# Group norm of a hybrid encoder: one square root for four token tiles, the middle tiles' statistics inside the last recurrence chunk, the bias folded into the bonus, and one more half gate in chunk 0

## The chip, the cores and the metric

The kernel runs on one core of one Trainium2 chip. The metric is the device time of one execution in microseconds (us), median of three runs. Five engines work beside each other, each through its own list of instructions in order: TensorE (PE in the rows, its weight loads PEld), VectorE (DVE), ScalarE (ACT), GpSimd (POOL) and SyncE (SP, which here only starts DMA transfers).

## The reference, cut to what matters

One encoder layer over 512 tokens of width 1024, in float32. The part that the change touches is the end of branch A, an RWKV-7 recurrence in both directions with 8 heads of 64 channels:

```python
y = rwkv7_scan(..., False) + rwkv7_scan(..., True)      # (tokens, heads, 64)
mean = jnp.mean(y, axis=-1, keepdims=True)
var = jnp.mean(jnp.square(y - mean), axis=-1, keepdims=True)
y = ((y - mean) * lax.rsqrt(var + GN_EPS)).reshape(B, S, W)
y = y * ln_w + ln_b
bonus = jnp.sum(jnp.sum(r_h[:, :, None] * k_dir * r_k, axis=-1, keepdims=True), axis=2) * v_h
y = (y + bonus.reshape(B, S, W)) * g                     # g = sigmoid(gd) @ g2
y_a = y @ w_o
merged = sigmoid(gate_A) * y_a + sigmoid(gate_B) * y_b   # y_b: differential attention
```

Behind it come the output projection, a feed-forward part of width 4096 and a gated embedding part.

## The kernel before

Products of float32 matrices are done in three matmuls of a split form (`whi`, `wlo` are the two halves of a weight unit of 128x1024; ACT makes the first at line 131, DVE the second at line 135). Weight units are loaded ahead, in order, into 3 raw and 4 split buffers.

The work runs in stages. **Preparation** (lines 297 to 551): projections of the input (`in`), and for each of four head pairs p and two directions d a chain from `zw`, `za` (matmuls) over ACT functions and DVE products (`ga`, `ae`, `bk`) to matmuls `aps` that need `bk`, and at the end of each p the bonus `bv` (line 536), which goes to DRAM as `bvd` and comes back later as `bvt`. The next stage's first matmuls (`da`) fill PE's waits from the last pair on. **Attention** follows with the first half of the gates (`gA`) and its projection (`yb`).

**The recurrence** (lines 1052 to 1154) works in 8 chunks of 64 tokens, both directions in step. A chunk has the matmuls `al`, a copy `B` by ACT and DVE, `ss` with B, a copy `srv` by ACT and DVE, `ss` with srv, the update of the state `S` by DVE, and `yy`, whose result is stored in `ya` (chunks 0 to 3, by ACT) or added to it (chunks 4 to 7, by DVE, line 1109). In the list of PE each small group waits for the copies before it. To give PE something in these waits, halves of the second gates `gB` (8 gates of 24 matmuls each, halves of 12) are put between by `fill`; a gate that is complete is drained on DVE and ACT (`gb`, line 1122; tanh; `mB`, line 1124), and the split of a further weight unit comes along with it:

```python
for i in range(NCH):
    steps = [step(i, d) for d in range(2)]
    for st_ in range(6):
        for g in steps:
            next(g)
        if st_ == 0 or (i, st_) == (0, 2):
            fill(1)
```

So 9 halves lie in the chunks, 2 of them in chunk 0, and the other 7 behind them (line 1200), where they run beside the group norm.

**The group norm** (lines 1164 to 1198) goes over four token tiles of 128: sum, mean, difference, square on ACT, sum, square root on ACT, reciprocal, product, and four transposes into `yps`. Then for each of four channel tiles: `yf` from yps with the scale `lnw` and the bias `lnb` on ACT (line 1191), the bonus added on DVE (line 1192), the product with the output gate `gq` (a matmul), and the split into `ygh` and `ygl`. These feed the projection `ya` (line 1211, weight units `wo`), whose PSUM bank is one of two that the gates use too: the first `ya` needs the bank of gate 6 and the second that of gate 7, so both need those gates' `gb`. Rows of DVE that add to the tile named ya (line 1109) and matmuls named ya (projection, lines 245 to 247) are different things.

The order on each engine is set by a scheduler when the kernel is built, from the program's order and priorities and its own estimates of when things are ready; `issue_after` pins an instruction behind another one on its engine.

Of the kernel before, what the change touches and what calls it, by code (L numbers as in the profile page):

```python
# [10 lines left out]
F32 = mybir.dt.float32  # L11
F32R = mybir.dt.float32r
AF = mybir.ActivationFunctionType
ALU = mybir.AluOpType
AX = mybir.AxisListType

P = 128
T = 512
D = 1024
C = 64  # L20
NCH = T // C
# [88 lines left out]
class Weights:  # L110
# [34 lines left out]
    def next(self, *key):  # L145
        assert UNITS[self.cur] == key, (UNITS[self.cur], key)
        self.prefetch(1 + self.AHEAD)
        w = self.ready[self.cur]
        self.ready[self.cur] = None
        self.cur += 1  # L150
        return w
# [3 lines left out]
def tile_hybrid_encoder(ctx, tc, xT, wts, par, cst_a, cst_p, lor, lqk, nfin, out, dbg=None):  # L155
    nc = tc.nc
# [4 lines left out]
    def pool(name, bufs=1, side=None, space=None):  # L161
        kw = {"reuse_waits": "tile"} if space != DR else {}
        if side:
            kw["side"] = side
        if space is not None:
            kw["space"] = space
        return Pool(tc.tile_pool(name=name, bufs=bufs, **kw))

    def dump(name, t, idx=None):
        if name in dbg:  # L170
            o = dbg[name]
            nc.sync.dma_start(o if idx is None else o[idx], t)
# [17 lines left out]
    eps6, epsg, sub8, lam = [one[:, i:i + 1] for i in range(4)]  # L190
# [4 lines left out]
    def par_col(name, i):  # L195
        return pr[:, POFF[name] + i:POFF[name] + i + 1]
# [167 lines left out]
    def tmp(tag, name, bufs=1):  # L364
        return pp.tile([P, T], F32, tag=tag, name=name, bufs=bufs)
# [8 lines left out]
    def proj_in(f, dst):  # L374
        shifted(proj(f), f, dst)
# [70 lines left out]
    for p in range(4):  # L446
# [87 lines left out]
        nc.tensor.matmul(bps, cp[:, CP["blk"]:CP["blk"] + P], rk, start=True, stop=True)  # L534
        bv = tmp("bv", f"bv{p}")
        nc.vector.tensor_tensor(bv, bps, v_, ALU.mult)
        nc.sync.dma_start(bvd[p], bv)
    proj_in(14, sgd)
    nc.scalar.activation(sgd, sgd, AF.Tanh, scale=0.5)
# [170 lines left out]
    def gate(f, pool_, stops):  # L710

        w = W.next("in", 3456 + f * P)
        ps = psd.tile([P, T], F32, tag="d", name=f"gA{f}")
        for k in range(8):
            wk = slice(k * P, k * P + P)
            for i, (a, b) in enumerate(((0, hhi), (0, hlo), (1, hhi))):
                chained(nc.tensor.matmul, ps, w[a][:, wk], moved(b[:, k, :]), start=(k == 0 and i == 0), stop=(k == 7 and i == 2))
            if k in stops and k < 7:
                yield
        late.append((f, ps, pool_))  # L720
        yield
# [3 lines left out]
    def gated():  # L725

        while late:
            f, ps, pool_ = late.pop()
            go = pool_.tile([P, T], F32, tag="go", name=f"go{f}", bufs=1)
            K(nc.vector.tensor_tensor, go, ps, rbs, ALU.mult)  # L730
            K(nc.scalar.activation, go, go, AF.Tanh, scale=0.5)
            nc.sync.dma_start(gad_[f], go)
# [283 lines left out]
    yp = pool("yp", side="right")  # L1016
    ya = yp.tile([P, 4, 8, C], F32, name="ya")
    bvt = yp.tile([P, 4, T], F32, name="bvt")
    sq_ = pool("seq", side="right")
# [8 lines left out]
    seq_last = None  # L1028
# [83 lines left out]
    def gate_b(f):  # L1112

        nonlocal last_pe
        w = W.next("in", 4480 + f * P)
        ps = psd.tile([P, T], F32, tag="d", name=f"gB{f}")
        last_pe = dense_half(w, ps, 0)
        yield
        last_pe = dense_half(w, ps, 1)
        gb = yp.tile([P, T], F32, tag="gb", name=f"gb{f}", bufs=1)  # L1120
        m_ = mB[f // 4][:, f % 4, :]
        nc.vector.tensor_tensor(gb, ps, rbs, ALU.mult)
        nc.scalar.activation(gb, gb, AF.Tanh, scale=0.5)
        nc.vector.scalar_tensor_tensor(m_, gb, 1.0, m_, ALU.add, ALU.mult)
        yield

    def dense_work():
        for f in range(GA0, 8):
            for _ in gate(f, yp, (3, 7)):
                gated()  # L1130
                yield
        for f in range(8):
            yield from gate_b(f)

    def fill(n):

        nonlocal seq_last
        for _ in range(n):
            if seq_last is None:
                next(dense)  # L1140
            else:
                with tc.issue_after(seq_last.ins):
                    next(dense)
            seq_last = last_pe

    dense = dense_work()
    for i in range(NCH):
        steps = [step(i, d) for d in range(2)]
        for st_ in range(6):
            for g in steps:  # L1150
                next(g)
            if st_ == 0 or (i, st_) == (0, 2):
                fill(1)
    with tc.issue_after(last_chunk.ins):
        nc.gpsimd.dma_start(bvt, bvd.rearrange("a q t -> q a t"))
    pss.close_()
# [3 lines left out]
    sq_ = yp  # L1160
# [2 lines left out]

    psm = pool("psm2", bufs=6, space=PS)

    mean = sq_.tile([P, 4, 8], F32, name="mean")
    var = sq_.tile([P, 4, 8], F32, name="var")
    g2 = sq_.tile([P, 512], F32, name="g2")
    with tc.issue_after(last_chunk.ins):
        nc.gpsimd.dma_start(g2, lor[:, 2, :])  # L1170
    gps = []
    yps = [psm.tile([P, T], F32, tag="m", name=f"yps{p}") for p in range(4)]
    for tt in range(4):
        yt = ya[:, tt]
        nc.vector.tensor_reduce(mean[:, tt, :], yt, AX.X, ALU.add)
        nc.vector.tensor_scalar(mean[:, tt, :], mean[:, tt, :], 1.0 / C, None, ALU.mult)
        nc.vector.tensor_tensor(yt, yt, mean[:, tt, :, None].broadcast_to([P, 8, C]), ALU.subtract)
        yq = sq_.tile([P, 8, C], F32, tag="yq", name=f"yq{tt}", bufs=2)
        nc.scalar.activation(yq, yt, AF.Square)
        nc.vector.tensor_reduce(var[:, tt, :], yq, AX.X, ALU.add)  # L1180
        nc.scalar.activation(var[:, tt, :], var[:, tt, :], AF.Sqrt, bias=epsg, scale=1.0 / C)
        nc.vector.reciprocal(var[:, tt, :], var[:, tt, :])
        nc.vector.tensor_tensor(yt, yt, var[:, tt, :, None].broadcast_to([P, 8, C]), ALU.mult)
        for p in range(4):
            nc.tensor.transpose(yps[p][:, tt * P:(tt + 1) * P], yt[:, 2 * p:2 * p + 2, :].rearrange("q h e -> q (h e)"), ident)
# [2 lines left out]
    ygl = mg.tile([P, 4, T], F32R, name="ygl")  # L1188
    for p in range(4):
        yf = sq_.tile([P, T], F32, tag="yf", name=f"yf{p}", bufs=2)  # L1190
        nc.scalar.activation(yf, yps[p], AF.Identity, bias=par_col("lnb", p), scale=par_col("lnw", p))
        nc.vector.tensor_tensor(yf, yf, bvt[:, p, :], ALU.add)
        gq = psm.tile([P, T], F32, tag="m", name=f"gq{p}")
        nc.tensor.matmul(gq, g2[:, p * P:(p + 1) * P], sgd, start=True, stop=True)
        nc.vector.tensor_tensor(yf, yf, gq, ALU.mult)
        dump("yg", yf, p)
        nc.scalar.activation(halves(ygh[:, p, :]), turns(yf), AF.Copy)
        nc.vector.tensor_tensor(halves(ygl[:, p, :]), turns(yf), halves(ygh[:, p, :].bitcast(F32)), ALU.subtract)
# [7 lines left out]
    for f2 in range(4):  # L1206
        w = W.next("wo", f2)
        for i in range(2):
            f = 2 * f2 + i
# [286 lines left out]
```

## Time and profile before

| what | us |
|---|---|
| median of 3 runs (lowest, highest) | 924.59 (922.39, 930.75) |
| the profiled execution: device time | 924.65 |
| the profiled execution: span of the trace | 922.5 |
| PE busy in the span | 879.3 |
| DVE busy | 572.0 |
| ACT busy | 430.7 |
| mean granted clock of PE (1 is full) | 0.985 |

The span is the time from the first to the last instruction; 2.1 us of the device time lie around it. Starts in the rows count from the beginning of the span. A bracket at the end of a row gives how long the engine stood idle before it and for what. A row of stretches gives start and end, the length, then busy time and in parentheses the number of instructions of PE, PEld, DVE, ACT and POOL, then PEclk, the busy share of the DMA engines, and GB/s. PEclk is the granted clock of PE: 1.00 is 2.4 GHz and 0.50 is 1.2 GHz.

### The profile page before, as it was taken

The page shows a single profiled execution, that of the slowest core. Times are in us where ns is not written, and L with a number is a line of the kernel's source. Part 1 is how long each engine was busy: PE and PEld are TensorE (multiplying, and loading weights), DVE is VectorE, ACT ScalarE, POOL GpSimd, SP SyncE. Part 2 cuts the span into 40 slices and gives each one's busy share as a digit, 9 for nine tenths or more (in the row PEclk, how much of TensorE's full clock was granted, in tenths as well). Part 3 has the DMA queues.
Part 4 walks back from the last instruction along what each step waited for, and adds up shares of the span by engine and source line. Part 5 has one row for each costly group of instructions (what it writes and reads, how often), then busy time and mean ns, then how long its engine had stood idle before and what let it go on. Part 6 is the DMA issues. An engine that isn't in the chain of part 4 may idle for free.

```text
span 922.5 us, 14089 instructions
## 1 busy us (share of the span) xinstructions
PE 879.3 (95%) x5640; PEld 738.1 (80%) x5640; DVE 572.0 (62%) x873; ACT 430.7 (47%) x677; POOL 57.2 (6%) x84
## 2 busy tenths in 40 slices
PE   5999898899999998999999999999999999999995
PEld 3788777788567787888877888888888888888884
DVE  7756999759996624567887655553454345435453
ACT  6665555453587534321654554542243234214555
POOL 5000000020000031332000000000000000000000
PEclk9999999999999999998999999999999999999998
DMA  6534787796237263786136223233232323233502
GB/s 216 190 115 148 249 271 259 244 358 209 92 148 176 82 178 115 260 256 230 47 107 224 91 92 111 95 101 106 95 111 93 114 92 114 92 108 98 206 24 91
DMA packets 64720, 138.57 MB, mean 150 GB/s; under 512 B 25808, under 2 KB 28112, under 8 KB 62352
## 3 DMA queue, kind: packets, MB, share of 16 engines
q1 hardware_dynamic: 59424, 110.68, 36.6%
q0 software_dynamic: 5232, 27.01, 8.8%
q8 instruction: 44, 0.72, 0.3%
q14 instruction: 20, 0.16, 0.1%
HBM read 106.73 MB, written 30.93 MB: 149 GB/s over the span
## 4 chain that ended last, share of the span: by engine, by line
PE 69%; DVE 16%; ACT 7%; DMA 4%; issue 3%; SPq 1%; POOLq 0%; DVEq 0%; ACTq 0%
PE f L246 12%; PE f L247 12%; PE f L245 12%; PE gA L655 4%; DVE wlo L135 2%; PE yb L655 2%; PE ss L1037 2%; PE yy L1037 2%; PE sc L655 2%; PE ov L655 2%; DMA md<-ga 1%; PE wout L246 1%; DVE mi L580 1%; ACT whi L131 1%; PE wout L245 1%
## 5 line engine op out<-in xcount | busy, mean ns | idle before, releaser
L131 ACT ACTIVATE whi<-raw 128x1024 fp32r<-128x1024 f32 x134 | 141.4, 1057 | 284.1 <-PE f L246 183.4
L135 DVE TENSOR_TENSOR wlo<-raw,whi 128x1024 fp32r<-128x1024 f32 x134 | 166.9, 1248 | 49.4 <-ACT whi L131 48.8
L247 PE MATMUL f<-fh,wlo 128*128 128x512 f32 x256 | 97.2, 380 | 0.0
L245 PE MATMUL f<-fh,whi 128*128 128x512 f32 x256 | 97.1, 379 | 0.0
L246 PE MATMUL f<-fl,whi 128*128 128x512 f32 x256 | 97.1, 379 | 0.0
L247 PE MATMUL f<-h1h,wlo 128*128 128x512 f32 x256 | 97.0, 379 | 0.0
L245 PE MATMUL f<-h1h,whi 128*128 128x512 f32 x256 | 97.0, 379 | 0.0
L246 PE MATMUL f<-h1l,whi 128*128 128x512 f32 x256 | 97.0, 379 | 0.0
L1273 DVE TENSOR_TENSOR x<-x,f 128x512 f32<-128x512 f32 x32 | 22.0, 688 | 89.5 <-PE f L247 89.5
L1262 DVE SCALAR_TENSOR_TENSOR ft<-f,rf 128x512 f32<-128x512 f32 x32 | 22.2, 693 | 62.8 <-PE f L247 62.7
L245 PE MATMUL in<-hhi,whi 128*128 128x512 f32 x128 | 50.8, 397 | 6.8 <-ACT whi L131 6.8
L245 PEld LDWEIGHTS f<-h1h,whi 128*128 128x128 f32 x256 | 48.4, 189 | 6.9
L246 PEld LDWEIGHTS f<-h1l,whi 128*128 128x128 f32 x256 | 48.4, 189 | 6.9
L247 PEld LDWEIGHTS f<-h1h,wlo 128*128 128x128 f32 x256 | 48.4, 189 | 6.9
L246 PEld LDWEIGHTS f<-fl,whi 128*128 128x128 f32 x256 | 48.4, 189 | 6.8
L245 PEld LDWEIGHTS f<-fh,whi 128*128 128x128 f32 x256 | 48.4, 189 | 6.8
L247 PEld LDWEIGHTS f<-fh,wlo 128*128 128x128 f32 x256 | 48.4, 189 | 6.8
L246 PE MATMUL in<-hlo,whi 128*128 128x512 f32 x128 | 51.2, 400 | 2.4 <-DVE hlo L301 2.4
L247 PE MATMUL in<-hhi,wlo 128*128 128x512 f32 x128 | 50.5, 395 | 1.1 <-DVE wlo L135 1.1
L245 PEld LDWEIGHTS in<-hhi,whi 128*128 128x128 f32 x128 | 25.4, 198 | 10.4 <-ACT whi L131 6.8
L1265 DVE TENSOR_TENSOR h1l<-ft,h1h 128x512 fp32r<-128x512 f32 x32 | 27.1, 846 | 8.1 <-ACT h1h L1264 8.1
L246 PEld LDWEIGHTS in<-hlo,whi 128*128 128x128 f32 x128 | 25.0, 195 | 8.1 <-DVE hlo L301 4.8
(365 smaller groups left out, 1835.5 us busy)
## 6 DMA issues: line engine op xcount, KB each, us to landing
raw<-in_wts_dram SPq DMA_DIRECT2D x134, 512.0 KB, 3.5
gad<-ga SPq DMA_DIRECT2D x16, 1024.0 KB, 5.6
sga<-gad POOLq DMA_DIRECT2D x16, 1024.0 KB, 7.8
xs<-in_xT_dram SPq DMA_DIRECT2D x8, 256.0 KB, 5.5
ppd<-pps SPq DMA_DIRECT2D x2, 1024.0 KB, 5.7
md<-ga SPq DMA_DIRECT2D x32, 64.0 KB, 4.8
gates<-go SPq DMA_DIRECT2D x8, 256.0 KB, 2.2
mi<-md POOLq DMA_DIRECT2D x1, 2048.0 KB, 11.6
```

What stands on the lines that cost most here:

```text
L131: a = nc.scalar.activation(hi, raw, AF.Copy)
L135: b = nc.vector.tensor_tensor(lo, raw, hi.bitcast(F32), ALU.subtract)
L245: nc.tensor.matmul(ps, lh, moved(rh), start=first, stop=False)
L246: nc.tensor.matmul(ps, lh, moved(rl), start=False, stop=False)
L247: return nc.tensor.matmul(ps, ll, moved(rh), start=False, stop=last)
L580: behind[e] = f(*args, **kw)
L655: last_pe = f(*args, **kw)
L1037: seq_last = nc.tensor.matmul(*args, **kw)
L1262: nc.vector.scalar_tensor_tensor(t_, ps, 0.0, rf, ALU.max, ALU.mult)
L1265: nc.vector.tensor_tensor(halves(hl_[:, f, :]), turns(t_), halves(hh_[:, f, :].bitcast(F32)), ALU.subtract)
L1273: nc.vector.tensor_tensor(x[:, f, :], x[:, f, :], ps, ALU.add)
```

## The change

Four things are done:

- The bias `lnb` is added to the bonus `bv` by ACT during preparation, before it goes to DRAM. Then scale and bonus are one DVE instruction (line 1210 of the changed kernel) in place of an ACT and a DVE instruction.
- The statistics (sum, mean, difference, square, sum of squares) of the middle token tiles 1 and 2, which are complete after chunk 5, are put into the program inside chunk 7; those of tiles 0 and 3 come after the chunks.
- One square root and one reciprocal serve all four tiles, where there were four of each.
- A third half of a gate lies in chunk 0, behind the step in which `srv` is copied; so 6 halves, and not 7, are left behind the chunks.

```diff
         bv = tmp("bv", f"bv{p}")
         nc.vector.tensor_tensor(bv, bps, v_, ALU.mult)
+
+        nc.scalar.activation(bv, bv, AF.Identity, bias=par_col("lnb", p))
         nc.sync.dma_start(bvd[p], bv)
...
+    mean = yp.tile([P, 4, 8], F32, name="mean")
+    var = yp.tile([P, 4, 8], F32, name="var")
+    yqs = {}
+
+    def statistics(tt, part):
+
+        yt = ya[:, tt]
+        if part == 0:
+            nc.vector.tensor_reduce(mean[:, tt, :], yt, AX.X, ALU.add)
+            nc.vector.tensor_scalar(mean[:, tt, :], mean[:, tt, :], 1.0 / C, None, ALU.mult)
+        elif part == 1:
+            nc.vector.tensor_tensor(yt, yt, mean[:, tt, :, None].broadcast_to([P, 8, C]), ALU.subtract)
+            yqs[tt] = yp.tile([P, 8, C], F32, tag="yq", name=f"yq{tt}", bufs=2)
+            nc.scalar.activation(yqs[tt], yt, AF.Square)
+        else:
+            nc.vector.tensor_reduce(var[:, tt, :], yqs[tt], AX.X, ALU.add)
...
-            if st_ == 0 or (i, st_) == (0, 2):
+            if st_ == 0 or (i, st_) in ((0, 2), (0, 3)):
                 fill(1)
+            if i == NCH - 1 and st_ in (2, 3, 4):
+
+                with tc.issue_after(seq_last.ins):
+                    for tt in (1, 2):
+                        statistics(tt, st_ - 2)
...
+    for part in range(3):
+        for tt in (0, 3):
+            statistics(tt, part)
+    nc.scalar.activation(var, var, AF.Sqrt, bias=epsg, scale=1.0 / C)
+    nc.vector.reciprocal(var, var)
     for tt in range(4):
         yt = ya[:, tt]
-        nc.vector.tensor_reduce(mean[:, tt, :], yt, AX.X, ALU.add)
...
-        nc.scalar.activation(var[:, tt, :], var[:, tt, :], AF.Sqrt, bias=epsg, scale=1.0 / C)
-        nc.vector.reciprocal(var[:, tt, :], var[:, tt, :])
         nc.vector.tensor_tensor(yt, yt, var[:, tt, :, None].broadcast_to([P, 8, C]), ALU.mult)
...
-        nc.scalar.activation(yf, yps[p], AF.Identity, bias=par_col("lnb", p), scale=par_col("lnw", p))
-        nc.vector.tensor_tensor(yf, yf, bvt[:, p, :], ALU.add)
+        nc.vector.scalar_tensor_tensor(yf, yps[p], par_col("lnw", p), bvt[:, p, :], ALU.mult, ALU.add)
```

On PE in chunk 0, before (digits behind a name are chunk and direction, or the gate's number; the number after the underscore is the tile's): 

```order
L1037 MATMUL ss00_3339<-B00_3317,stt0_3266 64x64 x8
L1037 MATMUL ss01_3351<-B01_3320,stt0_3266 64x64 x8
L1037 MATMUL ss00_3339<-srv00_2570,sga00_2280 64x64 x8
L1037 MATMUL ss01_3351<-srv01_2572,sga01_2282 64x64 x8
L1037 MATMUL yy00_3350<-srv00_2570,sga00_2280 64x64 x8
L1037 MATMUL yy01_3362<-srv01_2572,sga01_2282 64x64 x8
```

And now, on PE at the same place; the dots stand for the remaining ten matmuls of the half gate:

```order
L1039 MATMUL ss00_3345<-B00_3323,stt0_3270 64x64 x8
L1039 MATMUL ss01_3357<-B01_3326,stt0_3270 64x64 x8
L245 MATMUL gB1_3375<-hhi_79,whi43_3224 128x512
L246 MATMUL gB1_3375<-hlo_80,whi43_3224 128x512
...
L1039 MATMUL ss00_3345<-srv00_2574,sga00_2284 64x64 x8
L1039 MATMUL ss01_3357<-srv01_2576,sga01_2286 64x64 x8
```

Half of gate 1 has moved between the two groups of ss. Its second half follows at the start of chunk 1, so gates are now complete at the start of chunks 1, 3, 5 and 7, and no longer of 2, 4 and 6.

On DVE in chunk 6, before, from the additions of chunk 5 to the second copy srv:

```order
L1109 TENSOR_TENSOR ya_3258<-yy51_4099,ya_3258 64x4x64 x2
L1122 TENSOR_TENSOR gb3_4175<-gB3_4015,rbs_143 128x512
L1175 TENSOR_REDUCE mean_4441<-ya_3258 128x8 x2
L1124 SCALAR_TENSOR_TENSOR mB0_3134<-gb3_4175,mB0_3134 128x512
L1073 COPY B60_4213<-al60_4179 64x4x64
L1073 COPY B61_4216<-al61_4196 64x4x64
L1176 TENSOR_SCALAR mean_4441<-mean_4441 128x8 x2
L135 TENSOR_TENSOR wlo49_4556<-raw49_4554,whi49_4555 128x1024
L1081 COPY srv60_4154<-ss60_4219 64x4x64
L1177 TENSOR_TENSOR ya_3258<-ya_3258,mean_4441 128x512
L1081 COPY srv61_4160<-ss61_4239 64x4x64
```

And now, on DVE at the same place:

```order
L1111 TENSOR_TENSOR ya_3262<-yy51_4121,ya_3262 64x4x64 x2
L1156 TENSOR_REDUCE mean_3284<-ya_3262 128x8 x2
L1157 TENSOR_SCALAR mean_3284<-mean_3284 128x8 x2
L1159 TENSOR_TENSOR ya_3262<-ya_3262,mean_3284 128x512
L1075 COPY B60_4238<-al60_4204 64x4x64
L1159 TENSOR_TENSOR ya_3262<-ya_3262,mean_3284 128x512
L1075 COPY B61_4241<-al61_4221 64x4x64
L1083 COPY srv60_4176<-ss60_4244 64x4x64
L1163 TENSOR_REDUCE var_3285<-yq1_4440 128x8
```

The scheduler takes the middle tiles' statistics out of chunk 7 up into chunk 6, among the copies that PE waits for there; the drain of a gate and a weight split have left this chunk, and stand before the copies of chunk 7 now (gb, wlo and mB, in this order).

On PE in the last piece of preparation (pair 3, direction 1), before; the dots stand for fifteen further da matmuls:

```order
L362 MATMUL za31_1476<-lx_266,lwl_264 128x512
L247 MATMUL da01_1689<-whi21_1665,hlo_80 128x512
L245 MATMUL da00_1688<-whi21_1665,hhi_79 128x512
...
L246 MATMUL da01_1689<-wlo22_1672,hhi_79 128x512
L247 MATMUL da01_1689<-whi22_1671,hlo_80 128x512
L517 MATMUL aps3100_1507<-ga310_1497,bk31_1496 128x128
```

And now; the dots stand for five further da matmuls:

```order
L362 MATMUL za31_1479<-lx_266,lwl_264 128x512
L245 MATMUL da01_1693<-whi22_1675,hhi_79 128x512
L246 MATMUL da01_1693<-wlo22_1676,hhi_79 128x512
...
L246 MATMUL da01_1693<-wlo22_1676,hhi_79 128x512
L247 MATMUL da01_1693<-whi22_1675,hlo_80 128x512
L517 MATMUL aps3100_1510<-ga310_1500,bk31_1499 128x128
```

Through the added ACT instruction the scheduler's order of the preparation changes as well: projections and the first 48 da matmuls stand earlier among the waits of PE (33 and 31 dense matmuls before the two aps of pair 1, where there were 26 and 24), and 9, not 19, are left for the last wait.

## Rows read from the trace of the kernel before

**Rows 1.** The page, busy time of each engine and its share of the span:

```profile
PE 879.3 (95%) x5640; PEld 738.1 (80%) x5640; DVE 572.0 (62%) x873; ACT 430.7 (47%) x677; POOL 57.2 (6%) x84
```

**Rows 2.** Busy times by stretch: most of the preparation:

```profile
88.00:166.00 78.00, 70.66 (x466) 57.24 (x465) 76.77 (x126) 46.43 (x91) 0.00 (x0) 1.00 0.76 249
```

**Rows 3.** Timeline of PE: chunk 0's wait; starts of chunks 2, 3, 4, 6, 7; chunk 6's wait:

```profile
366.24 1.15 PE L1037 MATMUL ss<-srv,sga 128*64 128x64 f32 x32 [2.44 <-DVE srv L1081]
...
381.71 0.68 PE L1037 MATMUL al<-srv,sga 64*64 64x64 f32 x16
...
392.21 0.68 PE L1037 MATMUL al<-srv,sga 64*64 64x64 f32 x16
...
401.84 0.68 PE L1037 MATMUL al<-srv,sga 64*64 64x64 f32 x16
...
422.34 0.68 PE L1037 MATMUL al<-srv,sga 64*64 64x64 f32 x16
...
426.54 1.10 PE L1037 MATMUL ss<-B,stt 64*64 64x64 f32 x14 [0.99 <-DVE B L1073]
...
436.62 0.68 PE L1037 MATMUL al<-srv,sga 64*64 64x64 f32 x16
```

**Rows 4.** Timeline of DVE in chunk 0, a gate's drain ahead of the copies:

```profile
362.93 0.69 DVE L1122 TENSOR_TENSOR gb<-gB,rbs 128x512 f32<-128x512 f32 x1 [1.94 <-PE gB L247]
363.81 1.22 DVE L135 TENSOR_TENSOR wlo<-raw,whi 128x1024 fp32r<-128x1024 f32 x1 [0.18 <-ACT whi L131]
```

**Rows 5.** Timeline of DVE at the start of chunk 6: additions, then two sums:

```profile
421.80 1.73 DVE L1109 TENSOR_TENSOR ya<-yy,ya 64x256 f32<-64x256 f32 x4
...
424.16 1.27 DVE L1175 TENSOR_REDUCE mean<-ya 128x8 f32<-128x512 f32 x2
```

**Rows 6.** Stretches around waits of PE, with its granted clock:

```profile
172.00:178.00 6.00, 4.00 (x22) 3.22 (x22) 4.78 (x9) 3.24 (x7) 0.00 (x0) 1.00 0.96 322
245.00:250.00 5.00, 3.27 (x12) 1.63 (x11) 4.54 (x9) 2.88 (x6) 0.00 (x0) 0.91 0.79 248
250.00:255.00 5.00, 5.00 (x21) 3.33 (x20) 4.82 (x13) 3.60 (x10) 0.00 (x0) 0.75 0.19 78
428.00:432.00 4.00, 4.00 (x74) 3.77 (x72) 2.02 (x5) 0.43 (x2) 0.00 (x0) 0.50 1.01 379
```

**Rows 7.** Timeline of PE behind the chunks: gate matmuls, then the first two projections:

```profile
442.53 0.48 PE L245 MATMUL gB<-hhi,whi 128*128 128x512 f32 x1
...
443.07 0.38 PE L247 MATMUL gB<-hhi,wlo 128*128 128x512 f32 x1
443.28 0.38 PE L245 MATMUL gB<-hhi,whi 128*128 128x512 f32 x1
...
466.13 0.38 PE L245 MATMUL ya<-ygh,whi 128*128 128x512 f32 x1
...
470.44 0.48 PE L245 MATMUL ya<-ygh,whi 128*128 128x512 f32 x1 [1.24 <-DVE gb L1122]
```

**Rows 8.** Timeline of ACT in the group norm, a table load and the roots behind it:

```profile
446.49 1.15 ACT L1179 ACTIVATE yq<-ya 128x512 f32<-128x512 f32 x2 [0.22 <-DVE ya L1177]
447.65 1.28 ACT L1181 ACT_TABLE_LOAD   x1
448.95 0.49 ACT L1181 ACTIVATE var<-var,one 128x8 f32<-128x8 f32 x2
```

**Rows 9.** Groups of DVE by line, shapes apart: the group norm's instructions:

```profile
L1198 DVE TENSOR_TENSOR ygl<-yf,ygh 128x512 fp32r<-128x512 f32 x4 | 3.0, 802 | 0.4 <-ACT ygh L1197 0.4
...
L1192 DVE TENSOR_TENSOR yf<-yf,bvt 128x512 f32<-128x512 f32 x4 | 2.6, 688 | 0.0
...
L1183 DVE TENSOR_TENSOR ya<-ya,var 128x512 f32<-128x512 f32 x4 | 2.5, 675 | 0.0
```

**Rows 10.** Groups of ACT by line: scale and bias in one:

```profile
L1191 ACT ACTIVATE yf<-yps,pr 128x512 f32<-128x512 f32 x4 | 2.9, 764 | 0.0
```

**Rows 11.** Timeline of PE at its last wait in the preparation:

```profile
177.74 1.16 PE L517 MATMUL aps<-ga,bk 64*128 64x128 f32 x16 [2.00 <-DVE bk L499]
```

More of the change, by code (lines that the diff above doesn't have):

```diff
@@ L1164, in tile_hybrid_encoder @@
     psm = pool("psm2", bufs=6, space=PS)
-    mean = sq_.tile([P, 4, 8], F32, name="mean")
-    var = sq_.tile([P, 4, 8], F32, name="var")
     g2 = sq_.tile([P, 512], F32, name="g2")
@@ L1172, in tile_hybrid_encoder @@
     yps = [psm.tile([P, T], F32, tag="m", name=f"yps{p}") for p in range(4)]
+    for part in range(3):
[3 more added lines that the diff above has]
+    nc.vector.reciprocal(var, var)
     for tt in range(4):
         yt = ya[:, tt]
-        nc.vector.tensor_reduce(mean[:, tt, :], yt, AX.X, ALU.add)
[L1176 to L1180, printed above, removed]
-        nc.scalar.activation(var[:, tt, :], var[:, tt, :], AF.Sqrt, bias=epsg, scale=1.0 / C)
-        nc.vector.reciprocal(var[:, tt, :], var[:, tt, :])
         nc.vector.tensor_tensor(yt, yt, var[:, tt, :, None].broadcast_to([P, 8, C]), ALU.mult)
```

## The prediction

> **What bounds the kernel now.** I read the page's list of engines first: PE is busy 879.3 us of a span of 922.5, DVE 572.0, ACT 430.7 [rows 1]. So a piece of work that leaves PE, or a wait of PE that goes, counts in full, and what moves on DVE or ACT counts only where PE waits for it. The waits are local, so I then read the stages. In the preparation the stretches show DVE busy 76.77 us of 78 and PE 70.66 [rows 2]: here DVE sets the pace, and PE's waits are filled with da. In the recurrence PE's timeline gives the chunks: chunk 2, at whose start a gate is drained, takes 392.21 − 381.71 = 10.50 us, chunk 3, without a drain, 401.84 − 392.21 = 9.63, chunk 6 436.62 − 422.34 = 14.28 and chunk 7 442.53 − 436.62 = 5.91 [rows 3, 7]. Chunk 6 has a reason beside its drain: the granted clock is 0.50 from 428 to 432 [rows 6], that is 1.2 GHz in place of 2.4. Behind the chunks PE runs gate matmuls back to back from 442.53 to the first projection at 466.13 [rows 7], so the group norm is hidden beside them, except that the second projection waits 1.24 us for a gate's drain.
>
> **The half gate.** It moves, it does not go: PE has 24 × 8 gate matmuls in both kernels. Behind the chunks there are 72 now, not 84. Two neighbours start 0.21 to 0.22 us apart [rows 7], so 12 × 0.215 = 2.6 us leave that stretch, where PE has no idle time. In chunk 0 they stand before the first matmul that waited 2.44 us for srv [rows 3]: they fill that wait and overrun it by 2.6 − 2.44 = 0.2. Net −2.4. If the copy srv is still late behind them the gain is less; I see nothing that would delay it.
>
> **The drains.** A gate is now complete, and drained, at the start of chunks 1, 3, 5 and 7 and no longer 2, 4 and 6. A drain costs chunk 2 against chunk 3 10.50 − 9.63 = 0.87. Of chunks 1 to 5, two had one and three will: +0.9. In chunk 7 the drain is new: DVE does gb 0.69 and wlo 1.22 [rows 4] and mB, 0.69 as the same shape, before the copies B, 2.6 us in all, behind the additions of chunk 6. Between the last yy of a chunk and the need for B PE has a half gate of 2.6 and four groups al (0.68 each, a little overlapping [rows 3], some 2.4), and the additions take 1.73 [rows 5]. By that sum (1.73 + 2.6 + a copy of 0.43 against 5.0) nothing would wait; but the drain cannot begin before the gate's last matmul, which is PE's last before al, so 2.6 + 0.4 stand against 2.4 plus ACT's share of the copies. Bounds: 0.9, as any other drain, and 2.5, if gb, wlo and mB show almost whole. I take +1.4, nearer to the first, which is a row of the same thing.
>
> **Chunk 6.** Its drain goes and the middle tiles' sums come. DVE now does the additions, 1.73, two sums, 1.27 [rows 5], a scale, by estimate 0.2, and one difference, 0.68 as the product of its shape [rows 9], before copy B: 3.9 us, where it did additions, gb, sums and mB before, 4.4. The second difference stands between the two copies. So PE's wait here, 0.99 before [rows 3], stays about what it was: I take 9.63 for a chunk, 1.1 for the wait and 0.3 for sums and squares beside srv, 11.0. Before, 14.28 holds the drain chunk of 10.50, about 0.4 for additions that chunk 2 does not have on DVE, and so 3.4 of slow clock. At full clock the chunk goes from 14.28 to 11.0, −3.3 in all: +0.1 of work and −3.4 of clock. That the clock stays up is the step of which I am least sure; it is the first rival.
>
> **The group norm.** Removed are four ACT instructions of 0.764 [rows 10], three roots, three reciprocals and two of the table loads of 1.28 [rows 8]; four DVE additions of 0.688 [rows 9] become four instructions scalar_tensor_tensor, whose price no row shows with these inputs; 0.69 is the nearest of its kind (bounds 0.67 and 0.80, the group's shortest and longest). All that is ACT's and DVE's time beside PE, and worth nothing unless PE waits. Does it still not wait? Before, the roots of the first two tiles ended at 448.95 + 0.49 = 449.4 [rows 8], so a first product is ready some 0.3 + 0.675 later [rows 9], at 450.4. The same chain (additions, two sums, two differences, squares, sums, root) now serves tiles 0 and 3, since 1 and 2 are done. PE reaches the first transpose after 40 gate matmuls, 442.53 + 40 × 0.215 = 451.1: 0.7 us to spare. Four products follow at 0.675, and PE has four transposes and a gq between them at about the same pace. Then DVE has 4 × (0.69 + 0.675 + 0.802) = 8.7 us [rows 9] up to the last ygl, from about 453.5, while PE does 32 gate matmuls, 6.9, and what is left of gq: ygl is ready at 462.2, PE there at 461.7. The first projection takes its units in turn, so only its last needs the last ygl; but its bank waits for gb of gate 6, which stands behind that ygl on DVE: +0.4, my estimate from these two figures. The second projection's wait of 1.24 [rows 7] goes, since both gates are complete and drained one after the other before it. Net −0.8, with bounds of −1.2 (no wait at all) and +1.5 (the first waits for ygl, gb and a table load).
>
> One page speaks against me here. Before, a load takes 1.28 us and the roots start 0.02 behind it, 0.01 after the squares [rows 8]. The Trainium skill ("ScalarE: Activation LUTs", section "What ACT_TABLE_LOAD costs") says that a switch also holds a drain of about 1380 ns, 2.66 us in all. By the row nothing is added; by the page the single root would be 1.38 late and, 0.7 of it covered, some 0.7 to 1.2 would show in front of the transposes.
>
> **The preparation.** Four ACT additions of the bias are new: 4 × 0.764 = 3.1 us [rows 10], on an engine busy 46.43 of 78 [rows 2]. They stand behind bv and only the transfer to DRAM waits for each. I cost them at nothing, the cover being ACT's idle time; if one stands before a function of the chain it delays DVE by 0.76 (bounds −0.7, if the new order is luckier, and +1.1). But the order moves: 9 da matmuls, not 19, are left for the last wait of PE. It was 2.00 us at 177.74 [rows 11]; with ten fewer, 10 × 0.215 = 2.15 later at the wait, it is about 4.1. The work has only moved earlier, where it shortens other waits, and DVE sets the pace, so this is 0 by itself. The clock is the question. Around that wait of 2.00 it stayed 1.00 [rows 6]; but a stretch with PE busy 3.27 of 5 was followed by one at 0.75, half of it at 1.2 GHz [rows 6], so 2.5 us of slow clock cost 1.25, and in chunk 6 3.4. With a longer wait here I expect a fall, and take +1.7, half of 3.4, because DVE covers part of it; bounds 0 and 3.4.
>
> The Trainium skill ("TensorE: Matmul & The Clock Gate", section "Why this matters for your kernels") warns of idle gaps between bursts of matmuls in mid-kernel, after which the engine is back at half its rate. The wait of 2.00 without a fall [rows 6, 11] does not contradict it, as it was short; by the rule the gap of 4.1 would bring one, up to the 3.4 above.
>
> **The sum.** −2.4 (half gate) + 0.9 (drains) + 1.4 (chunk 7) + 0.1 (chunk 6) − 0.8 (norm) = −0.8; −3.4 of clock in chunk 6 gives −4.2; +1.7 of clock in the preparation gives −2.5. Against the profiled execution, 924.65 (922.5 of span and 2.1 around it; the median is 924.59, so no correction), that is 922.1. Most of what the change saves is not on PE's path, and of what is, half comes back as drains.
>
> **Rivals.** A: the clock falls neither in the preparation nor in chunks 6 and 7: 924.65 − 4.2 = 920.4. For it: a wait of 2.00 left it at 1.00. Against: the wait doubles.
>
> B, the slower side: chunk 6 or 7 keeps the slow clock. PE's wait for B is about as long as before, and chunk 7, of 5.91 us without a wait, gets one of its own. The saving of 3.4 is then not had: 922.1 + 3.4 = 925.5, 0.9 over now. It decides from a fall of about 2.5 us of cost in these two chunks.
>
> C: falls in both places and the whole 3.4 in the preparation, or norm and chunk 7 at their upper bounds (+2.3 and +1.1 over mine): 925.5 + 1.7 to 3.4, about 928.
>
> D: the single root is late, by the drain above or because ACT makes a weight half in front (128 × 1024 elements, so about the 1.15 of two squares [rows 8]): the transposes wait about 1.2, and 923.3.
>
> **How the numbers follow.** Forecast 0.42, A 0.17, B 0.25, C 0.10, D 0.06. A measurement of this kernel tells about 1% from no change, 915.4 and 933.8. Below 915.4 no sum of mine comes: A with every bound at its best (−0.7 in the preparation, −0.4 norm, −0.5 chunk 7) is 918.8; 0.05 for what I overlook. Above 933.8 is C with one more fall of 3.4 and a late chain: 0.05. The range goes from 918, below A, to 928, C's time.
>
> **What would show it.** Right: 72 gate matmuls behind chunk 7 and no wait at srv in chunk 0; chunks 3 and 5 at about 10.5 and 2 and 4 at 9.6; chunk 6 near 11.0 at a clock of 1.00, chunk 7 near 7.3; no wait before the second projection; a wait of some 4 us before the last aps, and a clock below 1.00 behind it. Wrong: a clock of 0.50 in chunk 6 or 7, the transposes waiting for the products, or a recurrence or preparation that takes longer at full clock.

## The result, and the profile after

The changed kernel takes 930.44 us (median of 17 runs), the kernel before 923.11 (17 runs beside them): 0.76% slower, ratio 1.0076 with a 95% interval of 1.0055 to 1.0097. The prediction was 922.1, with a range of 918 to 928. The profiled execution has a span of 927.1 us, 4.6 more than before. The page's list of engines after:

```profile
PE 878.3 (95%) x5640; PEld 738.6 (80%) x5640; DVE 571.1 (62%) x870; ACT 428.9 (46%) x672; POOL 58.3 (6%) x84
```

Against [rows 1] PE is busy 1.0 us less in a span 4.6 us longer: the time did not go into work but into waits of PE. Where they are is read from the starts of PE's instructions. Timeline of PE after, the waits first (the last `zw` and the last wait of the preparation, then a wait in the attention; the last `bps` of the preparation stands between the two waits), then the starts of chunks 2 to 7, the first gate matmul behind them, the first transpose and the first projection:

```profile
173.53 0.46 PE L361 MATMUL zw<-lx,lwh 128*128 128x512 f32 x1
...
180.75 1.79 PE L517 MATMUL aps<-ga,bk 64*128 64x128 f32 x16 [4.16 <-DVE bk L499]
...
185.57 1.02 PE L534 MATMUL bps<-kd,cp 128*128 128x512 f32 x2
...
211.91 3.25 PE L657 MATMUL qt<-ca,qk 128*128 128x128 f32 x14 [4.19 <-DVE qk L582]
...
389.47 0.68 PE L1039 MATMUL al<-srv,sga 64*64 64x64 f32 x16
...
399.11 0.68 PE L1039 MATMUL al<-srv,sga 64*64 64x64 f32 x16
...
409.60 0.68 PE L1039 MATMUL al<-srv,sga 64*64 64x64 f32 x16
...
419.66 0.68 PE L1039 MATMUL al<-srv,sga 64*64 64x64 f32 x16
...
430.57 0.68 PE L1039 MATMUL al<-srv,sga 64*64 64x64 f32 x16
...
441.81 0.68 PE L1039 MATMUL al<-srv,sga 64*64 64x64 f32 x16
...
450.50 0.59 PE L245 MATMUL gB<-hhi,whi 128*128 128x512 f32 x1
...
459.83 0.63 PE L1204 MATMUL yps<-ca,ya 128*128 128x128 f32 x4 [0.32 <-DVE ya L1202]
...
472.60 0.45 PE L245 MATMUL ya<-ygh,whi 128*128 128x512 f32 x1 [0.49 <-DVE gb L1124]
```

The last `bps` was at 181.00 before, so the preparation is 4.6 us longer (PE's timeline of before, the last `zw` and the last `bps`):

```profile
170.52 0.46 PE L361 MATMUL zw<-lx,lwh 128*128 128x512 f32 x1
...
181.00 1.02 PE L534 MATMUL bps<-kd,cp 128*128 128x512 f32 x2
```

Chunk 2 begins at 389.47 and not 381.71 [rows 3], 7.8 later: another 3.2 went in the attention and chunks 0 and 1. Chunks 2 to 7 take 450.50 − 389.47 = 61.0 where they took 60.8 [rows 3, 7]. From there to the first projection it is 22.1, not 23.6: −1.5; and from that to the end 454.5, not 456.4: −1.9, in which the wait of 1.24 [rows 7] is gone. 4.6 + 3.2 + 0.2 − 1.5 − 1.9 = 4.6, the whole difference of the spans. So the part of the program that the change is about did gain (−3.2 from chunk 2 on), and two stages that I had costed at +1.7 and nothing lost 7.8.

**The preparation.** DVE sets its pace, so the loss must be idle time or new work of DVE. Stretches of before (pair 1, then pair 3 up to the last bps), columns as in [rows 2]:

```profile
109.63:133.29 23.66, 21.45 (x147) 17.21 (x146) 23.40 (x39) 14.08 (x27) 0.00 (x0) 1.00 0.82 267
...
159.51:181.00 21.49, 19.24 (x140) 15.99 (x138) 18.60 (x33) 11.23 (x24) 0.00 (x0) 1.00 0.75 251
```

and the same two pieces after:

```profile
109.54:136.43 26.89, 24.43 (x161) 19.94 (x160) 25.46 (x41) 15.60 (x29) 0.00 (x0) 1.00 0.81 261
...
162.66:185.57 22.91, 18.02 (x127) 15.11 (x126) 16.85 (x29) 10.88 (x23) 0.00 (x0) 0.93 0.75 248
```

Pair 1 is 3.2 us longer. DVE does 25.46 − 23.40 = 2.1 more there (a weight split wlo and a product bv have come in from later), on an engine that had 0.3 us free, and then waits 1.26. All six profiles with the additions on ACT (the changed kernel and runs 2, 3, 4, 9 and 10) have 26.9 us for pair 1, the eight others 23.7 to 23.8. Pair 3 has 1.75 less of DVE's work and is still 1.4 longer: the free time is filled with waits. But it is longer only at its end. Up to its second zw it takes 173.53 − 162.66 = 10.87 us, before 170.52 − 159.51 = 11.01; from there to the end of PE's last wait 7.22 in both, 180.75 − 173.53 and 177.74 − 170.52 [rows 11]; and from there to bps 4.82, before 3.26. These 1.6 stand where the clock is 0.52, as shown below. Timeline of DVE after, both waits for ACT's sg:

```profile
124.57 1.23 DVE L480 TENSOR_TENSOR_SCAN en<-cp,sg 128x512 f32<-128x512 f32 x1 [1.26 <-ACT sg L474]
...
165.72 1.23 DVE L478 TENSOR_TENSOR_SCAN en<-cp,sg 128x512 f32<-128x512 f32 x1 [1.81 <-ACT sg L474]
```

Before the second stands one of the four new instructions, first in ACT's chain to sg. Before the first stands none: that chain begins behind a copy for which ACT waited on PE's xps, which now stands behind more dense matmuls. Timeline of ACT after, the copy, then the chain of pair 3:

```profile
122.26 0.60 ACT L523 ACTIVATE ga<-xps 128x512 f32<-128x512 f32 x1 [1.28 <-PE xps L522]
...
163.30 0.71 ACT L538 ACTIVATE bv<-bv,pr 128x512 f32<-128x512 f32 x1
163.92 0.68 ACT L471 ACTIVATE sg<-zw,hw 128x512 f32<-128x512 f32 x1
164.49 0.68 ACT L473 ACTIVATE th<-za,ha 128x512 f32<-128x512 f32 x1
165.06 0.63 ACT L474 ACTIVATE sg<-sg 128x512 f32<-128x512 f32 x1
```

So the addition can have put sg off by at most 163.92 − 163.30 = 0.6 us, in a piece that did not become longer; what that piece would take without it no run shows. What costs time in these rows is the order.

**The clock.** Stretches after: behind the wait of 4.16, behind that of 4.19, the end of chunk 7, and chunk 6, whose clock was 0.50 before [rows 6]:

```profile
181.00:184.00 3.00, 3.00 (x24) 2.44 (x24) 2.82 (x5) 0.38 (x1) 0.00 (x0) 0.52 0.10 21
...
212.00:215.00 3.00, 3.00 (x15) 3.00 (x16) 2.70 (x9) 3.00 (x4) 0.00 (x0) 0.50 1.05 433
447.50:450.50 3.00, 3.00 (x54) 2.76 (x52) 1.15 (x3) 0.38 (x1) 0.00 (x0) 0.50 0.01 5
430.60:441.80 11.20, 10.06 (x205) 8.65 (x204) 10.62 (x25) 2.54 (x7) 3.37 (x6) 1.00 0.89 291
```

Each of the two long waits has a stretch at 1.2 GHz behind it. Another one is at the end of chunk 7 (447.5 to 450.5), where no wait of PE is longer than 0.94; chunk 6 now runs at 2.4.

**The attention.** The wait of 4.19 before qt is for DVE's qk, and DVE was held by a small transfer, lq (128 KB), which stands a little ahead of it on DVE. Timeline after, of POOL and SP, which issue transfers, and of DVE; then the view of tile lq, from issue to landing:

```profile
193.51 0.68 POOL L616 DMA_DIRECT2D mi<-md  x1 [167.57 <-DMA bvd<-bv]
...
194.77 0.38 SPq L596 DMA_DIRECT2D lq<-in_lqk_dram  x1
...
209.78 0.36 DVE L599 TENSOR_TENSOR lq<-lq 128x64 f32<-128x64 f32 x2 [10.19 <-DMA lq<-in_lqk_dram]
```

```profile
DMA to landing us min/median/max: 15.0/15.0/15.0
```

and the same of before:

```profile
190.41 0.39 SPq L594 DMA_DIRECT2D lq<-in_lqk_dram  x1
...
190.90 0.68 POOL L614 DMA_DIRECT2D mi<-md  x1 [166.15 <-DMA bvd<-bv]
...
195.14 0.35 DVE L597 TENSOR_TENSOR lq<-lq 128x64 f32<-128x64 f32 x2
```

```profile
DMA to landing us min/median/max: 4.4/4.4/4.4
```

Before, SP issued lq 0.5 us ahead of POOL's 2 MB transfer mi, and it landed in 4.4 us. After, it was issued 1.3 us behind mi and took 15.0. SP issues it behind two weight units, and these wait for buffers that come free, by way of the splits, as PE does da matmuls. So a change of the order in the preparation turned a race between two queues round. The 3.0 us that this stage lost (185.57 to the start of chunk 0 at 366.56, before 181.00 to 358.96) hide some of it: the kernel before has two stretches at 1.2 GHz in the attention of its profile (0.95 is the mean granted clock from 248 to 318, after 1.00), 6.8 us in all against the 3.4 behind the wait for qt. Half of each taken off, the loss is 4.7, by estimate.

### The profile page after: what moved, and what is told of

Its sections match the earlier page's. It is cut to its first block, busy times and chain, and to the rows that moved or that the text cites. A ratio compares the mean times of both kernels' runs of the same rounds, so it can differ in the third digit from the quotient of the medians.

```text
span 927.1 us, 14076 instructions
## 1 busy us (share of the span) xinstructions
PE 878.3 (95%) x5640; PEld 738.6 (80%) x5640; DVE 571.1 (62%) x870; ACT 428.9 (46%) x672; POOL 58.3 (6%) x84
## 4 chain that ended last, share of the span: by engine, by line
PE 69%; DVE 16%; ACT 7%; DMA 4%; issue 3%; POOL 1%; SPq 0%; DVEq 0%; ACTq 0%; POOLq 0%
PE f L246 12%; PE f L247 12%; PE f L245 12%; PE gA L657 4%; DVE wlo L135 3%; PE yb L657 2%; DMA lq<-in_lqk_dram 2%; PE ss L1039 2%; PE ov L657 1%; PE in L245 1%; PE in L247 1%; PE in L246 1%; PE yy L1039 1%; ACT whi L131 1%; DVE mi L582 1%
## 5 line engine op out<-in xcount | busy, mean ns | idle before, releaser
L1280 DVE SCALAR_TENSOR_TENSOR ft<-f,rf 128x512 f32<-128x512 f32 x32 | 22.1, 691 | 61.2 <-PE f L247 61.2
L245 PEld LDWEIGHTS in<-hhi,whi 128*128 128x128 f32 x128 | 25.4, 198 | 10.4 <-ACT whi L131 6.8
```

Source lines behind the costliest of these rows:

```text
L245: nc.tensor.matmul(ps, lh, moved(rh), start=first, stop=False)
L1280: nc.vector.scalar_tensor_tensor(t_, ps, 0.0, rf, ALU.max, ALU.mult)
```

## The experiments

The theory after the first comparison: the bias addition in the preparation costs 7.8 us up to the recurrence (4.6 by the order into which the scheduler puts DVE's and PE's work there, and the rest because lq comes behind mi), and what was done to the norm gains about 3. The rival: the chunks and the norm lose, by the drain in chunk 7, the early statistics and slow clock there. Medians of a set are compared with runs of the kernel before on the same chip; its level moved by 3 us between sets (926.25, 923.64, 923.20), so ratios are used.

**1. Bias back in the norm.** The changed kernel with

```diff
-        nc.scalar.activation(bv, bv, AF.Identity, bias=par_col("lnb", p))
...
-        nc.vector.scalar_tensor_tensor(yf, yps[p], par_col("lnw", p), bvt[:, p, :], ALU.mult, ALU.add)
+        nc.scalar.activation(yf, yps[p], AF.Identity, bias=par_col("lnb", p), scale=par_col("lnw", p))
+        nc.vector.tensor_tensor(yf, yf, bvt[:, p, :], ALU.add)
```

> The changed kernel with the bias back in the group norm (ACT scale and bias, DVE addition) and not in the preparation; half gate, statistics and the single root stay. Main theory (the bias addition in the preparation costs the time: +4.6 up to the last bps and +3.0 behind it, where lq lands late; recurrence, norm and first projections together gain 3.1): the preparation is that of before again, the recurrence starts at 359 as before, and the run is about 3 us below before, some 920. Rival (the loss of the median, larger than in the one profile, comes from the drain in chunk 7, the statistics or slow clock there): the run stays above before, at 926 or more.

Measured: 923.23 us, ratio 0.9949 (0.9917 to 0.9980). Slower has become faster by one undone part. The pieces of the preparation are those of before to 0.02 us, the last wait is 2.00 again. lq is issued 0.2 us ahead of mi again and takes 7.4; DVE waits 2.3 for it, and PE does not wait for qt. The rival falls.

**2. Only the bias in the bonus.** The kernel before with the same edit the other way round:

```diff
+        nc.scalar.activation(bv, bv, AF.Identity, bias=par_col("lnb", p))
...
-        nc.scalar.activation(yf, yps[p], AF.Identity, bias=par_col("lnb", p), scale=par_col("lnw", p))
-        nc.vector.tensor_tensor(yf, yf, bvt[:, p, :], ALU.add)
+        nc.vector.scalar_tensor_tensor(yf, yps[p], par_col("lnw", p), bvt[:, p, :], ALU.mult, ALU.add)
```

> The kernel before with only the bias put into the bonus in the preparation and scale and bonus in one instruction. Main theory: the whole loss is here: last zw some 3 us later than before, last aps waiting some 4 us for bk with a slow clock behind it, lq landing some 15 us after its issue, recurrence 7 to 8 us later; the run is about 930. Rival: no later than 925.

Measured: 932.56 us, 1.0059 (1.0030 to 1.0088): the loss is here in full. Its PE timeline has both waits:

```profile
179.87 2.08 PE L517 MATMUL aps<-ga,bk 64*128 64x128 f32 x16 [4.16 <-DVE bk L499]
...
210.19 1.75 PE L656 MATMUL qt<-ca,qk 128*128 128x128 f32 x14 [2.52 <-DVE qk L581]
```

lq took 13.3 us from issue to landing, so the late lq comes with the bias and not with anything in the norm.

**3. lq on POOL.** The changed kernel with

```diff
-    nc.sync.dma_start(lq, lqk)
+    nc.gpsimd.dma_start(lq, lqk)
```

> The changed kernel with one edit: the transfer of lq is issued by POOL ahead of the 2 MB transfer mi, not by SP behind two weight units. PE's order is the same. Main theory (lq is overtaken by mi and shares the DMA engines with it, and PE waits 4.2 us for qt behind that): lq lands within some 5 us, the wait of 4.2 before qt goes, and the run is 3 to 4 us below the changed kernel, about 927. Rival (the late lq is a matter of the one profiled execution, or DVE is late there for another reason): within 1 us of the changed kernel's 930.4.

Measured: 924.75 us, 0.9974 (0.9947 to 1.0002). POOL issues it during the preparation, and it lands 4.3 us later (timeline of POOL, and the view of tile lq):

```profile
173.75 0.68 POOL L596 DMA_DIRECT2D lq<-in_lqk_dram  x1 [149.25 <-PE za L362]
```

```profile
DMA to landing us min/median/max: 4.3/4.3/4.3
```

The wait before qt is gone, and that of 1.7 before sc with it: from the last bps to chunk 0 it is 4.7 us shorter than in the changed kernel. But the ratio says about 9 us, more than expected, with sets of different level between; runs 9 and 10 settle it.

**4. No third half gate.** The changed kernel with

```diff
-            if st_ == 0 or (i, st_) in ((0, 2), (0, 3)):
+            if st_ == 0 or (i, st_) == (0, 2):
```

> The changed kernel without the third half gate in chunk 0. Main theory (the half gate gains 2.4 in chunk 0 and its drains cost some 0.3 to 0.9 in chunks 1 to 5 and about 1.1 in chunk 7): 0.5 to 2 us over the changed kernel, some 931.5, with a wait of about 2.4 for srv in chunk 0 and no drain in chunk 7. Rival (the drain in chunk 7 and its slow clock cost more than the half gate gains): 1 us or more below the changed kernel.

Measured: 932.40 us, 1.0061 (1.0031 to 1.0092), against 1.0076 with the half gate: the intervals overlap, so the times tell nothing. In the one profile the wait for srv in chunk 0 is back and the stretch from chunk 0 to the last projection is 130.0 us where the changed kernel has 126.4; 1.7 of that is one more stretch at 1.2 GHz, by estimate, and 1.9 is left for the half gate:

```profile
374.29 1.98 PE L1039 MATMUL ss<-srv,sga 128*64 128x64 f32 x32 [2.44 <-DVE srv L1083]
```

That stretch comes with this wait: the clock is 0.50 from 373.6 to 376.9. It is 0.50 there in runs 2 and 7 too, which have the same wait, though not in the profile of the kernel before. The prediction counted the wait alone.

**5. Bias on POOL.** The changed kernel with

```diff
-        nc.scalar.activation(bv, bv, AF.Identity, bias=par_col("lnb", p))
+        nc.gpsimd.tensor_scalar(bv, bv, par_col("lnb", p), None, ALU.add)
```

> The changed kernel with the four bias additions of the preparation on POOL in place of ACT; they still stand between bv and its transfer. PE's order in the preparation is then that of before (26, 24, 30, 31, 29, 19 dense matmuls before the aps). Main theory (not the addition itself costs the time, but the order into which it makes the scheduler put PE's dense matmuls): pair 1 takes 10.96 + 12.70 us again from zw to zw, the last wait for bk is 2.0 again with no slow clock behind it, and the run is 3 to 5 us below before, as with the bias in the norm. Rival (the extra step between bv and its transfer, or its engine time, is what delays): pair 1 or the last piece stays longer by a us or more.

Measured: 922.21 us, 0.9977 (0.9950 to 1.0004): some 2 us below before and not the 3 to 5 expected, and the interval holds no change too. With the same additions, and the same place in front of the transfer, PE's order is that of before, and so are the two pieces to 0.1 us (stretches), with POOL's new work in the sixth column; then PE's last wait (timeline):

```profile
110.35:134.10 23.75, 21.46 (x148) 17.22 (x146) 23.49 (x39) 14.08 (x27) 1.57 (x1) 1.00 0.82 266
...
160.30:181.85 21.55, 19.30 (x139) 15.99 (x138) 18.66 (x33) 11.29 (x24) 1.56 (x1) 1.00 0.75 250
```

```profile
178.59 1.16 PE L517 MATMUL aps<-ga,bk 64*128 64x128 f32 x16 [2.01 <-DVE bk L499]
```

Additions of 1.57 on POOL cost at most 0.1 us in each of the two pieces where those of 0.71 on ACT cost 4.6 in all. lq took 4.1 us, though SP still issues it, 0.14 behind mi; in the changed kernel and runs 2, 4 and 9 it is 0.7 to 2.1 behind. So both losses hang on the addition standing on ACT, with the order that comes of it. No run has the additions on ACT in the order of before, so the two were not separated by a run; by the rows above the addition in front of sg accounts for 0.6 us at most.

**6. Bias in the norm and lq on POOL.** The edits of 1 and 3 together.

> The changed kernel with the bias back in the norm and with lq issued by POOL ahead of mi: both causes of the loss taken away, half gate, statistics and single root kept. Main theory: the gain of the bias in the norm (0.5% below before) and in the attention another 2, since the wait of 1.7 before sc goes, as it did with lq on POOL alone: 0.7% below before, some 6 to 7 us. Rival (the two edits remove the same wait): 0.5%, as with the bias in the norm alone.

Measured: 920.37 us, 0.9979 (0.9956 to 1.0003). No gain over run 1 can be told, by the intervals; the rival is the nearer.

**7. Before, with lq on POOL.** The edit of 3 alone, in the kernel before.

> The kernel before with lq issued by POOL ahead of mi, nothing else. There lq lands 4.4 us after its issue and DVE does not wait for it. If the late lq is only the changed kernel's trouble: within 1 us of before. If lq on POOL also takes the wait of 1.73 before sc away, which the kernel before has: 1.5 to 2.5 us below before.

Measured: 922.73 us, 1.0002 (0.9972 to 1.0032): nothing. The wait before sc is gone in this profile, and it bought no time that the runs show. Where lq is in time, issuing it earlier gains nothing that can be told.

**8. Before, with the third half gate and lq on POOL.** The edit of 3, and that of 4 the other way round, in the kernel before.

> The kernel before with the third half gate in chunk 0 and lq on POOL; statistics, roots and bias as before. Main theory (of the change only the half gate gains, some 1.9 us net of the clock, and statistics and the single root gain about nothing): 3 to 5 us below before, and within 1.5 us of the run with bias in the norm and lq on POOL. Rival (the statistics in the chunks and the single root are worth 2 us or more): that much slower than it.

Measured: 923.30 us, 0.9995 (0.9965 to 1.0025). Not 3 to 5 us below before: the expectation fails. It is not told from run 6 (0.9979) either.

**9 to 12. Once more, side by side.** The changed kernel without an edit (9); with the edit of 3 (10); with those of 3 and 5 (11); and the kernel before with only the third half gate, the edit of 4 the other way round (12).

> The changed kernel as it is, measured beside the next three on one chip, since the level of the kernel before moved by some 3 us from one set of runs to the next. Main theory: again about 0.7% over before; pair 1 12.4 + 14.5 us, last wait 4.16 with a slow clock, lq 13 to 15 us from issue to landing and PE waiting 2.5 to 4.2 for qt. Rival (the late lq is chance): lq lands within 8 us and the run is 4 us less.

Measured: 932.47 us, 1.0103 (1.0073 to 1.0133). lq took 15.0 us, and PE waited 4.17 for qt; the clock fell behind both waits (stretches):

```profile
180.50:183.50 3.00, 2.83 (x20) 2.53 (x20) 2.80 (x7) 0.00 (x0) 0.00 (x0) 0.50 0.37 98
211.00:214.00 3.00, 2.36 (x11) 2.36 (x12) 2.73 (x11) 3.00 (x5) 0.00 (x0) 0.51 1.01 425
```

> The changed kernel with lq issued by POOL ahead of mi, once more, beside the changed kernel itself. Main theory: 5 us less than the changed kernel, of which the attention's 4.7 is the wait for lq. Rival: 9 us less, as the two ratios of the first sets would have it; then something beside the wait for qt has gone too.

Measured: 924.30 us, 1.0004 (0.9984 to 1.0025), 8.2 below the run before it. The rival's 9 is the nearer: something beside the wait goes. By the estimate that follows it is slow clock. The median granted clock of these runs is 0.9835 in the changed kernel and 0.988 with lq on POOL (0.989 before). Span times clock, an estimate of the span with no slow clock in it, gives medians of 915.4, 911.1 and 911.2: so of the 8.2 some 4.4 is the wait, and the rest slow clock. In the two profiles the piece from the last bps to chunk 0 differs by 3.1, with 10.2 us at 1.2 GHz in each. The stretch behind the wait for qt (0.51 in the rows of run 9) lasts 3.4 us and costs 1.7; where the other 2 of slow clock comes from is not shown.

> The changed kernel with lq issued by POOL and the four bias additions on POOL. Against lq_on_pool_again only the scheduler's order of the preparation differs (dense matmuls before the aps 26, 24, 30, 31, 29, 19 in place of 33, 31, 30, 29, 27, 9). Main theory (that order costs 3.2 in pair 1 and some 1.5 of slow clock at the last wait): 3 to 5 us less than lq_on_pool_again, about 0.6% below before. Rival (what the order loses in the preparation is given back in the attention): within 1 us of lq_on_pool_again.

Measured: 920.80 us, 0.9975 (0.9955 to 0.9996), 3.5 below the run before it, as the theory had it: what the order loses in the preparation is not given back. Against before it is 0.25%, not the 0.6 expected. Beside run 1 it is the only version whose interval lies below 1.

> The kernel before with only the third half gate in chunk 0. Main theory (the half gate is what gains of the change): about 2 us below before, chunk 0 at 12.4, chunk 7 with a drain at about 7 without slow clock, 1.9 less from chunk 0 to the last projection. Rival (its drain in chunk 7 takes the gain): within 1 us of before.

Measured: 922.84 us, 0.9991 (0.9969 to 1.0012). The rival's, but not by its mechanism. Chunk 7 takes 8.8 with slow clock in it, as in the changed kernel, and 12 gate matmuls fewer lie behind it; but now the norm is not ready, and the first projection waits twice (PE timeline of this run; run 8 has the same two waits, 0.43 and 1.08):

```profile
463.88 0.48 PE L245 MATMUL ya<-ygh,whi 128*128 128x512 f32 x1 [0.45 <-ACT ygh L1197]
...
465.47 0.48 PE L246 MATMUL ya<-ygl,whi 128*128 128x512 f32 x1 [1.10 <-DVE ygl L1198]
```

The changed kernel has neither, and its first projection waits only for gb, 0.49. From chunk 0 to the last projection this profile has 127.7, before 129.6, run 4 130.0 and the changed kernel 126.4. With half of the slow stretches taken off, by estimate (6.8 us of them in before and in run 4, 3.4 in the other two), these are 126.0, 126.2, 126.6 and 124.7: by them each half of the change alone would gain next to nothing, both together 1.5. The other runs do not bear that out. Run 7, whose program from chunk 0 on is that of before, gives 127.5 by the same reading, 1.3 more than before. And the estimate of run 10 gives a median of 909.7 for run 12 against 911.2 for before in its set, and 909.6 for run 8 against 911.0: the half gate alone gains some 1.5 by it. With the shorter norm it is 1.6 (run 6, 909.4 against 911.0) or 2.8 (run 1, 909.0 against 911.8), and in the changed kernel the half gate gains nothing by it (915.5 with, 915.2 without in run 4). Which part of the change gains, and whether the one needs the other, stays open.

## Why the prediction was wrong

Two steps failed: the new order of the preparation was put at 0 and cost 3.2 us, and the attention had no term and lost 3.0. The largest gain, 3.4 us of clock in chunk 6, for the most part came back as slow clock and a drain in chunk 7. By the prediction's own steps:

- **Half gate.** Right in its place: no wait for srv in chunk 0, and 72 gate matmuls behind the chunks. I had taken the half gate's −2.4 and the norm's −0.8 as two gains to be added. In runs 8 and 12, which have the half gate without the shorter norm, the first projection waits 1.5 for the norm, so part of the first gain can be lost; what each is worth was not settled.
- **Drains.** Right where I looked: chunk 2 takes 9.64 now and chunk 3 10.49, the 9.63 and 10.50 of [rows 3] exchanged. The size was not: chunks 1 to 5 together take 51.6 us, before 51.3, so +0.3 and not +0.9, since chunk 1 takes 10.54 with a drain and took 10.67 without.
- **Chunk 6.** 11.24 at a clock of 1.00; forecast 11.0 and a clock that stays up.
- **Chunk 7.** 8.69, forecast 7.3. At full clock it takes 7.4 (runs 6 and 10); the rest is a clock of 0.50 that half of rival B foresaw. The drain was sized rightly, the clock was not: the two chunks together went from 20.2 to 19.9, −0.3 and not −3.3 + 1.4 = −1.9. The profiles agree: in the four without the third half gate chunk 6 takes 12.8 to 14.3 and chunk 7 5.9 to 6.5, in the ten with it 10.4 to 11.3 and 7.4 to 9.0. The slow clock moved on to chunk 7, half as long in these two profiles (6.8 us before, 3.4 now).
- **Group norm.** The first projection waits 0.49 (forecast 0.4) and the second no longer. The new instruction of DVE takes 0.74 (forecast 0.69, bounds 0.67 and 0.80). Of a drain behind the table load, rival D's first reason, nothing shows: the load begins at 456.95 and takes 1.28, and the root follows at 458.25, 0.02 behind it. Its second reason is there, a weight half of ACT in front:

```profile
455.88 1.06 ACT L131 ACTIVATE whi<-raw 128x1024 fp32r<-128x1024 f32 x1 [0.52 <-PE gB L246]
456.95 1.28 ACT L1198 ACT_TABLE_LOAD   x1
458.25 0.32 ACT L1198 ACTIVATE var<-var,one 128x32 f32<-128x32 f32 x1
```

  The transposes wait 0.32, where I had 0.7 us to spare and rival D a wait of 1.2.
- **The last wait and its clock.** 4.16, forecast 4.1; the wait itself costs nothing (7.22 from zw to its end in both), and the clock falls behind it, as expected: 1.6, forecast 1.7. The rule that spoke against the change was borne out: the Trainium skill ("TensorE: Matmul & The Clock Gate", section "Why this matters for your kernels") warns of idle gaps in mid-kernel, and behind the 4.16 and the 4.19 the profile shows 0.52 and 0.50, where behind 2.00 [rows 6, 11] it stayed 1.00.
- **The preparation's order: the step that failed.** "The work has only moved earlier, where it shortens other waits, and DVE sets the pace, so this is 0 by itself": it was +3.2, in pair 1. In a stage where DVE is 98% busy, work of DVE that moves from pair 3 into pair 1 lengthens pair 1 by all of it (2.1 us) and makes idle time in pair 3, which nothing uses; the wait of 1.26 for sg comes on top. I had counted the da matmuls of PE that moved, and not the wlo and bv that moved on DVE with them. These 3.2 and the 1.6 of clock, less 0.2 in between, are the 4.6. The other sentence, "I cost them at nothing, the cover being ACT's idle time", with an upper bound of +1.1, holds for the additions as work on ACT: one of them stands directly before the three instructions that end in sg, for which DVE waits, but that piece takes 10.87 and took 11.01.
- **The attention: not looked at, and so a second step that failed.** The sum has no term for it. I followed each new wait on ACT and DVE, but not what SP's queue does next. I had looked at bvd's transfer and not at what stands three places behind it. lq, in time by 0.5 us before, was late by 10, and cost some 4.4 us and slow clock (runs 9 and 10). The Trainium skill ("DMA: Bandwidth & Descriptors", section "Issuing engines are not separate DMA queues") states that transfers started by SP and by POOL run on the same 16 DMA engines and interleave, so a queue of its own does not protect lq; 4.4 us where it is issued 0.5 ahead of mi against 13.3 to 15.0 where it is issued 0.7 to 2.1 behind agrees.

So, in the profiled execution, −4.2 forecast for recurrence and norm became −3.0, and +1.7 ahead of them +7.6: 3.2 in pair 1, 1.6 of clock behind the last wait, 3.0 up to chunk 0, less 0.2. The medians are 7.3 apart and the profiled executions only 4.5 (929.11 and 924.65), since that of the changed kernel lies 1.3 below its median and that of before 1.5 above.

## What to carry to other kernels

An instruction added on an engine with idle time can cost more than its own time: where a scheduler orders the program, it can change the lists of the other engines. Compare the bounding engine's own order stage by stage, since work that moves into a full stage costs its whole time, and the stage it leaves gives nothing back. Follow the DMA queues too: a small load that a stage needs at its start should be issued by a queue, and at a time, that no large transfer can overtake. And a stretch of slow clock that a change takes out of one place can come back at the next one, as here from chunk 6 to chunk 7, so it should not be booked whole as a gain.

## What was not expected of the hardware

A transfer of 128 KB landed 4.4 us after its issue when 0.5 us ahead of a transfer of 2 MB, and 13.3 to 15.0 us after it when 0.7 to 2.1 us behind (the changed kernel and runs 2, 4 and 9); within 0.2 us of it, on either side, it took 4.1 to 7.4 (runs 1, 5 and 12). An addition of 128x512 took 1.57 us on POOL against 0.71 on ACT, and DVE, 99% busy beside it, took 0.09 us more for the same work (23.49 against 23.40). And taking away one wait of 4.2 us took 8.2 off the median (runs 9 and 10), though the fall of the clock behind that wait explains 1.7 of the difference at most.
